# Moving the token and weight forms, the first residual adds and a late load in the block of 1024 tokens

## Chip, core and metric

The kernel runs on one core of a Trainium2 chip, as one program. The metric is the device time of one execution in microseconds, taken as the median of several runs. The engines are TensorE (PE, matrix products), VectorE (DVE), ScalarE (ACT), GpSimd (POOL) and SyncE (SP); each works through its own queue of instructions in order. Transfers are issued from SP's and POOL's queues.

## What is computed

The kernel is one block of a bidirectional encoder over 2048 tokens and 16 meta tokens of width 1024: attention and a Fourier mix from one input projection, then the part that matters here, a feed-forward net with a residual and a last norm:

```python
m = rms_norm(h, g_mlp[i])
h = h + jnp.square(jax.nn.relu(m @ w_up[i])) @ w_down[i]      # w_up 1024x4096, w_down 4096x1024
return rms_norm(h, g_final)[:, N_META:]
```

All of it is float32. A product of two float32 matrices is made from three products of halves: each operand is split into a rounded high half and a low remainder, and high x high, high x low and low x high are summed in PSUM.

## The kernel before

A split (`Split.__call__`) is two instructions: a cast on ACT that makes the high half (line 65) and a subtraction on DVE that makes the low half (line 66). `mm3` issues the three products (lines 75 to 77). So every operand of PE passes through ACT and then DVE. In the names below `h` and `l` stand for the halves: `ah`, `al` of activations, `wh_dn`, `wl_dn` of down weights, `wuh`, `wul` of up weights, `bfh`, `bfl` (or `bf` for both) of tokens, and in the down phase `bh`, `bl` of down weights.

The tokens are worked in blocks. The feed-forward net of blocks 0 and 1 (512 tokens each) runs in 8 groups of 512 hidden units: `up(b, grp)` makes four tiles of activations, each with a relu and a square on ACT and a split; `down(b, grp, halves)` multiplies them with four weight tiles for each half of the output and adds the four PSUM banks (`pdn`) to the residual rows `h` on DVE. The down weights come through a ring of three raw tiles (`wr`).

The last 1024 tokens are one block with another scheme: the 2x2 block product is done with seven products instead of eight, in the order `ORDER = "1265734"`. Operands are sums and differences of quarters ("forms"). On the weights' side the generator `up_weights()` yields the forms of one group of 512 hidden units: 1 and 2 straight from the loaded tiles R0 and R1, 6 and 5 from the sums `us2` and `us1`, 7 from a difference written in R0, then 3 and 4. On the tokens' side `b_form(name, ...)` splits the quarters `b11`, `b21`, `b12`, `b22` or differences of them (`minus`) once for all groups. The quarters come from `flips()`, which transposes the normalised rows through PSUM (`pmt`), with evictions on ACT (line 1107).

The transition into this block (lines 1154 to 1181) writes: `up(1, 7)` with the transposes between its steps, then four forms of the first weights, `b_form` 1 and 2, the first half of `down(1, 7)`, forms 5, the second half, forms 6, the last norm of block 1, and forms 7, 3 and 4. Then comes the up phase, 8 groups of seven products (`ux`, `uy`); `keep` stores activations and their sums to `s_d` in DRAM through SP (line 1220). After it the down phase runs 4 groups of seven products (`dx`, `dy`). Its operands come from `down_operands()`, two forms ahead: `a` forms from `s_d` (`stationary`), `b` forms from `w_down` (`load`), in the first group through POOL's queue and later through SP's. After the products of each form, `add(t)` adds four banks to the residual rows `hs` on DVE (line 1411). `load_h(i)` loads four residual rows of 512 KB each (line 1194); the second four (`hs1`) are first added to at form 5. The forms of products 6 and 7 continue in the same banks as product 1, so a bank's add must be done before its next product.

A scheduler of the tile framework sets the order on each engine, from the order in which the code is written and from when it reckons that inputs are there. `tc.issue_after(ins)` makes what is written inside it stand behind the instruction `ins` in the queue of `ins`'s engine.

Of the kernel before, what the change touches and what calls it, by code (L numbers as in the profile page):

```python
# [2 lines left out]

# [1 line left out]

# [7 lines left out]
AF = mybir.ActivationFunctionType  # L13
ALU = mybir.AluOpType
# [4 lines left out]
P = 128  # L19
# [32 lines left out]
def f32v(ap):  # L52
    return ap.bitcast(F32)


class Split:
# [5 lines left out]
    def __call__(self, hi, lo, src, scale=None):  # L62
        nc = self.nc
        if scale is None:
            nc.scalar.copy(hi, src)  # L65
            nc.vector.tensor_tensor(lo, src, f32v(hi), op=ALU.subtract)  # L66
        else:
            nc.scalar.activation(hi, src, AF.Copy, scale=scale)  # L68
            nc.vector.scalar_tensor_tensor(lo, src, scale, f32v(hi), op0=ALU.mult, op1=ALU.subtract)


def mm3(nc, out, a, b, first, last, chain=False):
# [7 lines left out]
def ins_of(x):  # L80
    return getattr(x, "ins", x)
# [49 lines left out]
def encoder_block(ctx: ExitStack, tc: tile.TileContext, x, meta, w_in, w_f,  # L131
                  w_out, w_up, w_down, g_fin, g_cols, g_rows, c_id, c_rope, c_dft, c_even, c_odd, c_rem, out):
    nc = tc.nc
# [281 lines left out]
    def drain(*gens):  # L415
        gens = list(gens)
        while gens:
            for g in list(gens):
                try:
                    next(g)  # L420
                except StopIteration:
                    gens.remove(g)
# [48 lines left out]
    for j in range(LAST + 1):  # L471
# [16 lines left out]
        else:  # L488
# [11 lines left out]
            a = 0  # L500
# [620 lines left out]
    def b_form(name, tiles, src):  # L1121

        BF[name] = tuple([t[:, i] for t in half for i in range(t.shape[1])] for half in tiles)
        k = 0
        for hi, lo in zip(*tiles):
            n = hi.shape[1]
            split(hi, lo, src[:, k:k + n])
            k += n
# [25 lines left out]
    fl = flips()  # L1154
    for _ in up(1, 7):
        next(fl, None)
    drain(fl)
    UW = up_weights()
    ready = [next(UW) for _ in range(4)]
    b_form("1", in_ey(0), b11)  # L1160
    b_form("2", in_ey(1), b21)
    drain(down(1, 7, (0,)))
    minus(b11, b12, b11)
    minus(b22t, b22, b11)
# [22 lines left out]

    FIRST = []
    hs = []

    def load_h(i):
        HS = ey.tile([P, 4, D], F32, name=f"hs{i}", tag=f"e{i}")
# [23 lines left out]
    for g in range(8):  # L1216
        X, Y, p1, u2, p5, C = ({} for _ in range(6))

        def keep(name, p, t):
            nc.sync.dma_start(s_d[g // 2][:, ORDER.index(name), 2 * (g % 2) + p], t)  # L1220

        for name in ORDER:
            hi, lo = ready.pop(0)
# [140 lines left out]
            yield form("4", t4)  # L1364

    gfin = [dn.tile([P, 512], F32, name=f"gf{i}", tag=f"gf{i}") for i in range(2)]
    for i in range(2):
        nc.sync.dma_start(gfin[i], g_fin[i * 512:(i + 1) * 512].rearrange("(o d) -> o d", o=1).broadcast_to([P, 512]))
    junks = [dn.tile([P, 512], F32, name=f"ej{i}", tag=f"ej{i}") for i in range(2)]
    DO = down_operands()  # L1370
    ready = [next(DO)]
    load_h(1)
    halves = (slice(0, 512), slice(512, 1024))
    sums = [small.tile([P, 2], F32, name=f"ess_{t}", tag="hss", bufs=8) for t in range(8)]
    WHERE = {"1": (0, 0), "2": (0, 0), "6": (0, 1), "5": (4, 1), "7": (4, 1), "3": (0, 1), "4": (4, 0)}
# [13 lines left out]
    for g in range(4):  # L1389
        X, Y = {}, {}  # L1390
        last = g == 3
        for name in ORDER:
# [20 lines left out]
            if not (last and name == "4"):  # L1413
                for t in range(4):
                    products(t)
                if "b" not in RING:
                    sp.release()
                    dr = Lines(tc.alloc_tile_pool(name="dr", bufs=1, side="right", reuse_waits="tile"), small)
                    RING["b"] = dr, 10
                    ready.append(next(DO))  # L1420
                w = next(DO, None)
                if w is not None:
                    ready.append(w)
                for t in range(4):
                    add(t)
                    if last and name == "2":
                        square(t, 0)
                    if last and name in "73":
                        square(o0 + t, 1)
                    if last and name == "3":  # L1430
                        store(t)
            else:
                for t in range(4):
                    products(t)
                    add(t)
                    square(4 + t, 0)
                    store(4 + t)
# [105 lines left out]
```

## Time and profile before

| | us |
|---|---|
| median of 3 runs | 2359.55 |
| lowest and highest | 2357.9, 2360.73 |
| the profiled execution | 2355.83 |
| its span, first to last instruction | 2354.0 |
| mean granted clock of TensorE, share of full | 0.991 |

The profile gives for each engine when it was busy and, where it stood idle, what it waited for. PE is the engine to look at first here. The part that the change touches begins at about 1690 us (second block's last group), the up phase of the last block runs from about 1709 to 2043 us, and its down phase from there to the end.

### The profile page before, as it was taken

The numbers are of one execution on the slowest core, as the hardware profiler recorded it, in microseconds if no ns is written. First come the engines' busy times: TensorE is split into PE (matmuls) and PEld (weight loads), VectorE is DVE, ScalarE is ACT, GpSimd is POOL, SyncE is SP. The second block draws the span as 40 slices with busy tenths as digits, with TensorE's granted clock in tenths as the row PEclk, the third lists the DMA queues.
The fourth block names the chain that finished last, engine by engine and source line by source line (L and its number), as shares of the span: only waits on it lengthen the run. The fifth ranks groups of instructions, "written<-read, shape, count | busy, mean of one in ns | idle before, by whom it ended". The sixth has DMA issues, their size and how long they took to land. (4 is left out here: it accounts for less than half of the span.)

```text
span 2354.0 us, 30528 instructions
## 1 busy us (share of the span) xinstructions
PE 2301.2 (98%) x10790; PEld 1882.8 (80%) x10790; DVE 1738.9 (74%) x2803; ACT 1292.8 (55%) x2427; POOL 173.6 (7%) x211
## 2 busy tenths in 40 slices
PE   8999989999899999999999999999999999999998
PEld 7889877677678888788878788888778888788886
DVE  5435668988877976977887987885695646597786
ACT  6434345544575655765675665664665555453333
POOL 2212120001110000200000000000000000100000
PEclk9999999999899999999999999999999999999999
DMA  6334152334543222433242353223534444865442
GB/s 212 103 106 118 46 168 68 113 114 147 187 123 100 85 81 68 122 120 109 70 151 86 112 193 105 72 81 126 179 112 170 144 165 152 318 199 164 129 134 81
DMA packets 173418, 302.08 MB, mean 128 GB/s; under 512 B 14688, under 2 KB 59456, under 8 KB 173136
## 3 DMA queue, kind: packets, MB, share of 16 engines
q1 hardware_dynamic: 154928, 259.49, 33.7%
q0 software_dynamic: 18336, 40.64, 5.8%
q8 instruction: 85, 1.39, 0.2%
q14 instruction: 69, 0.57, 0.1%
HBM read 226.37 MB, written 73.70 MB: 127 GB/s over the span
## 5 line engine op out<-in xcount | busy, mean ns | idle before, releaser
L75 PE MATMUL pdn<-wh_dn,ah 128*128 128x512 f32 x512 | 201.0, 394 | 2.7 <-ACT ah L65 2.7
L75 PE MATMUL pup<-mT,wh_up 128*128 128x512 f32 x512 | 201.7, 395 | 0.6 <-ACT mT L68 0.6
L76 PE MATMUL pdn<-wl_dn,ah 128*128 128x512 f32 x512 | 200.6, 392 | 0.0
L76 PE MATMUL pup<-mT,wh_up 128*128 128x512 f32 x512 | 200.4, 391 | 0.0
L77 PE MATMUL pup<-mT,wl_up 128*128 128x512 f32 x512 | 199.6, 392 | 0.0
L77 PE MATMUL pdn<-wh_dn,al 128*128 128x512 f32 x512 | 199.4, 391 | 0.0
L733 ACT ACTIVATE S<-S 128x512 f32<-128x512 f32 (+1 forms) x260 | 161.3, 630 | 59.8 <-DVE S L727 59.5
L691 ACT COPY S<-s 128x512 f32<-128x512 f32 (+1 forms) x272 | 158.2, 584 | 63.8 <-PE s L77 58.9
L727 DVE TENSOR_TENSOR S<-S,mb 128x512 f32<-128x512 f32 (+1 forms) x272 | 180.9, 683 | 11.9 <-ACT mb L720 11.8
L698 DVE TENSOR_TENSOR M<-M,S 128x512 f32<-128x512 f32 (+1 forms) x240 | 164.8, 687 | 32.2 <-ACT S L691 30.0
L65 ACT CAST wh_up<-wr_up 128x512 fp32r<-128x512 f32 x128 | 79.2, 622 | 152.8 <-PE pup L76 80.5
L66 DVE TENSOR_TENSOR wl_up<-wr_up,wh_up 128x512 fp32r<-128x512 f32 x128 | 87.6, 687 | 75.0 <-ACT wh_up L65 72.7
L65 ACT CAST wh_dn<-wr_dn 128x512 fp32r<-128x512 f32 x128 | 79.5, 621 | 93.4 <-PE pdn L77 50.1
L66 DVE TENSOR_TENSOR pl<-S,ph 128x512 fp32r<-128x512 f32 x180 | 123.4, 686 | 9.0 <-ACT ph L65 8.2
L75 PE MATMUL s<-q,kt 128*128 128x512 f32 (+1 forms) x272 | 126.6, 466 | 2.2 <-ACT S L691 1.2
L754 DVE TENSOR_TENSOR acc<-acc,S 128x512 f32<-128x512 f32 x180 | 123.1, 684 | 0.6 <-ACT S L733 0.2
L65 ACT CAST ah<-a 128x1024 fp32r<-128x1024 f32 x56 | 58.4, 1048 | 112.9 <-issue 62.1
L65 ACT CAST ph<-S 128x512 fp32r<-128x512 f32 x180 | 111.1, 618 | 16.8 <-PE o L77 8.1
L66 DVE TENSOR_TENSOR wl_dn<-wr_dn,wh_dn 128x512 fp32r<-128x512 f32 x128 | 87.4, 686 | 43.6 <-ACT wh_dn L65 36.8
L75 PEld LDWEIGHTS pdn<-wh_dn,ah 128*128 128x128 f32 x512 | 96.5, 189 | 25.4 <-ACT ah L65 3.1
L75 PEld LDWEIGHTS pup<-mT,wh_up 128*128 128x128 f32 x512 | 96.6, 189 | 20.4 <-ACT mT L68 1.0
L77 PEld LDWEIGHTS pdn<-wh_dn,al 128*128 128x128 f32 x512 | 96.5, 188 | 20.1
(315 smaller groups left out, 6375.5 us busy)
## 6 DMA issues: line engine op xcount, KB each, us to landing
wr_up<-in_w_up_dram SPq DMA_DIRECT2D x128, 256.0 KB, 2.8
wr_dn<-in_w_down_dram SPq DMA_DIRECT2D x128, 256.0 KB, 2.6
a<-s_d SPq DMA_DIRECT2D x42, 512.0 KB, 3.7
R<-in_w_up_dram SPq DMA_DIRECT2D x16, 1024.0 KB, 5.2
s_d<-s SPq DMA_DIRECT2D x64, 256.0 KB, 2.1
d<-in_w_down_dram SPq DMA_DIRECT2D x26, 512.0 KB, 4.9
s_d<-c SPq DMA_DIRECT2D x48, 256.0 KB, 2.0
h<-h_d SPq DMA_DIRECT2D x20, 512.0 KB, 5.6
```

Source lines behind the costliest of these rows:

```text
L65: nc.scalar.copy(hi, src)
L66: nc.vector.tensor_tensor(lo, src, f32v(hi), op=ALU.subtract)
L75: nc.tensor.matmul(out, a[0], b[0], start=first, stop=False, skip_group_check=chain)
L76: nc.tensor.matmul(out, a[0], b[1], start=False, stop=False, skip_group_check=chain)
L77: nc.tensor.matmul(out, a[1], b[0], start=False, stop=last, skip_group_check=chain)
L691: nc.scalar.copy(S[:rows], ps[:rows])
L698: nc.vector.tensor_tensor(M[:rows], M[:rows], S[:rows], op=ALU.max)
L727: nc.vector.tensor_tensor(S, S, s["mb"][:rows], op=ALU.subtract)
L733: nc.scalar.activation(p, S, AF.Exp, scale=ISQ)
L754: nc.vector.tensor_tensor(acc, acc, p, op=ALU.add)
```

## The change

There are three parts. First, the third and fourth form of the first weights (6 and 5, with their sums) and the token forms 1 and 2 are queued behind the last split of `up(1, 7)`: behind its cast in ACT's queue and behind its subtraction in DVE's. `Split` keeps its last two instructions for that. The first two forms stay as they were, and `acts_done` is taken before the remaining transposes are written. Second, `load_h(1)` and the loads of the last gain are queued behind the last `keep` store of the up phase, in SP's queue. Third, in the first down group the adds of products 1, 2 and 6 are queued behind the subtraction of the newest operand split.

```diff
--- before.py
+++ after.py
@@ -1,5 +1,5 @@
 import math
-from contextlib import ExitStack
+from contextlib import ExitStack, nullcontext
 
 import numpy as np
 
@@ -62,11 +62,12 @@
     def __call__(self, hi, lo, src, scale=None):
         nc = self.nc
         if scale is None:
-            nc.scalar.copy(hi, src)
-            nc.vector.tensor_tensor(lo, src, f32v(hi), op=ALU.subtract)
+            a = nc.scalar.copy(hi, src)
+            b = nc.vector.tensor_tensor(lo, src, f32v(hi), op=ALU.subtract)
         else:
-            nc.scalar.activation(hi, src, AF.Copy, scale=scale)
-            nc.vector.scalar_tensor_tensor(lo, src, scale, f32v(hi), op0=ALU.mult, op1=ALU.subtract)
+            a = nc.scalar.activation(hi, src, AF.Copy, scale=scale)
+            b = nc.vector.scalar_tensor_tensor(lo, src, scale, f32v(hi), op0=ALU.mult, op1=ALU.subtract)
+        self.last = ins_of(a), ins_of(b)
 
 
 def mm3(nc, out, a, b, first, last, chain=False):
@@ -1154,11 +1155,14 @@
     fl = flips()
     for _ in up(1, 7):
         next(fl, None)
+    UW = up_weights()
+    acts_done = split.last
     drain(fl)
-    UW = up_weights()
-    ready = [next(UW) for _ in range(4)]
-    b_form("1", in_ey(0), b11)
-    b_form("2", in_ey(1), b21)
+    ready = [next(UW) for _ in range(2)]
+    with tc.issue_after(acts_done[0]), tc.issue_after(acts_done[1]):
+        ready += [next(UW) for _ in range(2)]
+        b_form("1", in_ey(0), b11)
+        b_form("2", in_ey(1), b21)
     drain(down(1, 7, (0,)))
     minus(b11, b12, b11)
     minus(b22t, b22, b11)
@@ -1187,6 +1191,7 @@
 
     FIRST = []
     hs = []
+    kept = []
 
     def load_h(i):
         HS = ey.tile([P, 4, D], F32, name=f"hs{i}", tag=f"e{i}")
@@ -1217,7 +1222,7 @@
         X, Y, p1, u2, p5, C = ({} for _ in range(6))
 
         def keep(name, p, t):
-            nc.sync.dma_start(s_d[g // 2][:, ORDER.index(name), 2 * (g % 2) + p], t)
+            kept[:] = [ins_of(nc.sync.dma_start(s_d[g // 2][:, ORDER.index(name), 2 * (g % 2) + p], t))]
 
         for name in ORDER:
             hi, lo = ready.pop(0)
@@ -1364,12 +1369,12 @@
             yield form("4", t4)
 
     gfin = [dn.tile([P, 512], F32, name=f"gf{i}", tag=f"gf{i}") for i in range(2)]
-    for i in range(2):
-        nc.sync.dma_start(gfin[i], g_fin[i * 512:(i + 1) * 512].rearrange("(o d) -> o d", o=1).broadcast_to([P, 512]))
     junks = [dn.tile([P, 512], F32, name=f"ej{i}", tag=f"ej{i}") for i in range(2)]
     DO = down_operands()
     ready = [next(DO)]
-    load_h(1)
+    with tc.issue_after(kept[-1]):
+        load_h(1)
+        load_gfin(2, gfin)
     halves = (slice(0, 512), slice(512, 1024))
     sums = [small.tile([P, 2], F32, name=f"ess_{t}", tag="hss", bufs=8) for t in range(8)]
     WHERE = {"1": (0, 0), "2": (0, 0), "6": (0, 1), "5": (4, 1), "7": (4, 1), "3": (0, 1), "4": (4, 0)}
@@ -1421,8 +1426,10 @@
                 w = next(DO, None)
                 if w is not None:
                     ready.append(w)
+                behind = split.last[1]
                 for t in range(4):
-                    add(t)
+                    with tc.issue_after(behind) if g == 0 and name in "126" else nullcontext():
+                        add(t)
                     if last and name == "2":
                         square(t, 0)
                     if last and name in "73":
```

ACT's queue at the last activations of block 1, before (`r_1_7_f` are the tiles of activations, `ah_1_7_f` their casts; `wuh6` and `wuh5` are weight forms, `bf0` is token form 1):

```order
L65 CAST ah_1_7_0_16519<-r_1_7_0_16516 128x512
L65 CAST wuh6_0_16560<-us2_0_16557 128x1024
L964 ACTIVATE r_1_7_1_16523<-pup_1_7_1_16265 128x512
L65 CAST wuh5_0_16564<-us1_0_16556 128x1024
L1107 ACTIVATE b22_16262<-pmt_3_6_16504,cols_94 128x512
L1107 ACTIVATE b22_16262<-pmt_3_7_16510,cols_94 128x512
L965 ACTIVATE r_1_7_1_16523<-r_1_7_1_16523 128x512
L65 CAST bf0_16568<-b11_16259 128x1024
L65 CAST ah_1_7_1_16526<-r_1_7_1_16523 128x512
```

and after:

```order
L65 CAST ah_1_7_0_16519<-r_1_7_0_16516 128x512
L965 ACTIVATE r_1_7_1_16523<-pup_1_7_1_16265 128x512
L65 CAST wh_dn_1_7_0_2_16624<-wr_dn_1_7_0_2_16622 128x512
L966 ACTIVATE r_1_7_1_16523<-r_1_7_1_16523 128x512
L65 CAST wh_dn_1_7_0_3_16642<-wr_dn_1_7_0_3_16640 128x512
L1108 ACTIVATE b22_16262<-pmt_3_6_16504,cols_94 128x512
L1108 ACTIVATE b22_16262<-pmt_3_7_16510,cols_94 128x512
L65 CAST ah_1_7_1_16526<-r_1_7_1_16523 128x512
```

The casts of forms 6, 5 and 1 have left the place between `ah_1_7_0` and `ah_1_7_1`; two casts of down weights have come in.

DVE's queue at the same place, before (`al_1_7_f` are the low halves of the activations):

```order
L66 TENSOR_TENSOR wl_dn_1_7_0_1_16607<-wr_dn_1_7_0_1_16604,wh_dn_1_7_0_1_16606 128x512
L1088 TENSOR_TENSOR us1_0_16556<-R0_0_16544,R1_0_16546 128x1024
L66 TENSOR_TENSOR wul2_0_16553<-R1_0_16546,wuh2_0_16552 128x1024
L1089 TENSOR_TENSOR us2_0_16557<-us1_0_16556,R0_0_16544 128x1024
L1092 TENSOR_TENSOR R0_0_16544<-R0_0_16544 128x4x256
L66 TENSOR_TENSOR al_1_7_0_16520<-r_1_7_0_16516,ah_1_7_0_16519 128x512
L66 TENSOR_TENSOR wul6_0_16561<-us2_0_16557,wuh6_0_16560 128x1024
L66 TENSOR_TENSOR wul5_0_16565<-us1_0_16556,wuh5_0_16564 128x1024
L1094 TENSOR_TENSOR us2_0_16557<-R1_0_16546,us2_0_16557 128x1024
L66 TENSOR_TENSOR bf0_16568<-b11_16259,bf0_16568 128x1024
L66 TENSOR_TENSOR al_1_7_1_16527<-r_1_7_1_16523,ah_1_7_1_16526 128x512
```

and after:

```order
L66 TENSOR_TENSOR wl_dn_1_7_0_1_16607<-wr_dn_1_7_0_1_16604,wh_dn_1_7_0_1_16606 128x512
L66 TENSOR_TENSOR wul2_0_16553<-R1_0_16546,wuh2_0_16552 128x1024
L66 TENSOR_TENSOR al_1_7_0_16520<-r_1_7_0_16516,ah_1_7_0_16519 128x512
L66 TENSOR_TENSOR wl_dn_1_7_0_2_16625<-wr_dn_1_7_0_2_16622,wh_dn_1_7_0_2_16624 128x512
L66 TENSOR_TENSOR wl_dn_1_7_0_3_16643<-wr_dn_1_7_0_3_16640,wh_dn_1_7_0_3_16642 128x512
L66 TENSOR_TENSOR al_1_7_1_16527<-r_1_7_1_16523,ah_1_7_1_16526 128x512
L66 TENSOR_TENSOR al_1_7_2_16534<-r_1_7_2_16530,ah_1_7_2_16533 128x512
L66 TENSOR_TENSOR al_1_7_3_16541<-r_1_7_3_16537,ah_1_7_3_16540 128x512
L1089 TENSOR_TENSOR us1_0_16556<-R0_0_16544,R1_0_16546 128x1024
L66 TENSOR_TENSOR bf0_16568<-b11_16259,bf0_16568 128x1024
L1090 TENSOR_TENSOR us2_0_16557<-us1_0_16556,R0_0_16544 128x1024
L66 TENSOR_TENSOR bf0_16568<-b11_16259,bf0_16568 128x1024
```

The sums `us1`, `us2`, the difference in R0, the subtractions of forms 6 and 5 and those of `bf0` and `bf1` now stand behind `al_1_7_3`; the difference in R0 and the second use of `us2` stand further back still, behind the differences for form 6 and among the last norm's products. On PE, ten products of form 5 (`uy5`) now stand ahead of the products of the second output half's low weights, where before they came later. From the first product that reads `bf7_3` to the first product of the second group there are 66 matmuls on PE in the new order.

DVE's queue at the start of the down phase, before (`hs0` are the first four residual rows, `al2`, `bl2` and so on the operands of form 2; line 1330 makes differences of weights):

```order
L1411 TENSOR_TENSOR hs0_19023<-hs0_19023,dx_0_0_19181 128x512
L1411 TENSOR_TENSOR hs0_19023<-hs0_19023,dx_0_1_19194 128x512
L1411 TENSOR_TENSOR hs0_19023<-hs0_19023,dx_0_2_19207 128x512
L66 TENSOR_TENSOR al2_0_0_19161<-a2_0_0_19152,ah2_0_0_19160 128x1024
L1411 TENSOR_TENSOR hs0_19023<-hs0_19023,dx_0_3_19220 128x512
L66 TENSOR_TENSOR al2_0_1_19163<-a2_0_1_19154,ah2_0_1_19162 128x1024
L66 TENSOR_TENSOR bl2_0_0_19240<-d21_0_0_19156,bh2_0_0_19239 128x1024
L66 TENSOR_TENSOR bl2_0_1_19242<-d21_0_1_19158,bh2_0_1_19241 128x1024
L1411 TENSOR_TENSOR hs0_19023<-hs0_19023,dy2_0_0_19291 128x512
L1330 TENSOR_TENSOR d11_0_0_19164<-d12_0_0_19249,d11_0_0_19164 128x1024
```

and after:

```order
L66 TENSOR_TENSOR bl2_0_0_19240<-d21_0_0_19154,bh2_0_0_19239 128x1024
L66 TENSOR_TENSOR bl2_0_1_19242<-d21_0_1_19156,bh2_0_1_19241 128x1024
L1335 TENSOR_TENSOR d11_0_0_19162<-d12_0_0_19249,d11_0_0_19162 128x1024
L1335 TENSOR_TENSOR d11_0_1_19164<-d12_0_1_19251,d11_0_1_19164 128x1024
L1335 TENSOR_TENSOR t2_0_0_19261<-d22_0_0_19253,d11_0_0_19162 128x1024
L1335 TENSOR_TENSOR d12_0_0_19249<-d22_0_0_19253,d12_0_0_19249 128x1024
L1335 TENSOR_TENSOR t2_0_1_19262<-d22_0_1_19255,d11_0_1_19164 128x1024
L66 TENSOR_TENSOR bl6_0_0_19276<-t2_0_0_19261,bh6_0_0_19275 128x1024
L66 TENSOR_TENSOR al6_0_0_19272<-a6_0_0_19257,ah6_0_0_19271 128x1024
L66 TENSOR_TENSOR bl6_0_1_19284<-t2_0_1_19262,bh6_0_1_19283 128x1024
L66 TENSOR_TENSOR al6_0_1_19280<-a6_0_1_19259,ah6_0_1_19279 128x1024
L1416 TENSOR_TENSOR hs0_19023<-hs0_19023,dx_0_0_19181 128x512
```

The splits of form 2 stand ahead of all adds, and so do the differences and splits of form 6. In POOL's queue the loads of `a5` and `a7`, which wait for buffers that `al2` frees, keep their order.

## Rows read from the trace of the kernel before

**Rows 1.** The page, part 1: busy time of each engine, its share of the span, number of instructions.

```profile
PE 2301.2 (98%) x10790; PEld 1882.8 (80%) x10790; DVE 1738.9 (74%) x2803; ACT 1292.8 (55%) x2427; POOL 173.6 (7%) x211
```

**Rows 2.** The waits of PE, all from 1640 to 2344 us: engine, product and line, what it waited for, then us in total, times, longest.

```profile
PE pdn L75 <- ACT ah L65: 2.7, 1, 2.7
PE dy L76 <- DVE bl L66: 2.1, 1, 2.1
PE dx L75 <- ACT ah L65: 1.9, 1, 1.9
PE ux L76 <- DVE bf L66: 0.8, 1, 0.8
```

**Rows 3.** The timeline of PE around the largest wait: start us, duration us, engine, line, operation, output<-inputs, how many in a row; in brackets the idle time before it and what ended it.

```profile
1702.00 0.39 PE L77 MATMUL pdn<-wh_dn,al 128*128 128x512 f32 x1
1705.07 0.79 PE L75 MATMUL pdn<-wh_dn,ah 128*128 128x512 f32 x1 [2.68 <-ACT ah L65]
...
1708.75 0.40 PE L75 MATMUL pdn<-wh_dn,ah 128*128 128x512 f32 x1
```

**Rows 4.** Windows of 10 us: stretch, its length, busy us (and instructions) of PE, PE's weight loads, DVE, ACT and POOL, then granted TensorE clock, busy share of the DMA engines, GB/s.

```profile
1700.00:1710.00 10.00, 7.32 (x30) 5.64 (x29) 9.86 (x11) 10.00 (x16) 0.00 (x0) 0.83 0.00 0
1710.00:1720.00 10.00, 10.00 (x46) 8.25 (x46) 10.00 (x13) 8.20 (x17) 0.00 (x0) 1.00 0.16 54
1740.00:1750.00 10.00, 9.09 (x39) 6.92 (x38) 9.39 (x11) 4.26 (x6) 1.52 (x2) 1.00 0.45 156
2040.00:2050.00 10.00, 7.86 (x35) 6.17 (x34) 6.12 (x7) 0.00 (x0) 1.07 (x2) 1.00 1.04 415
2050.00:2060.00 10.00, 8.27 (x37) 6.51 (x35) 8.51 (x10) 2.95 (x4) 0.00 (x0) 1.00 0.35 137
```

**Rows 5.** The timeline of ACT ahead of the cast that ended the wait of the third group (columns as there).

```profile
1698.88 0.61 ACT L65 CAST ah<-r 128x512 fp32r<-128x512 f32 x1
1699.39 1.05 ACT L65 CAST wuh<-us 128x1024 fp32r<-128x1024 f32 x1
1700.34 0.60 ACT L964 ACTIVATE r<-pup 128x512 f32<-128x512 f32 x1
1700.83 1.05 ACT L65 CAST wuh<-us 128x1024 fp32r<-128x1024 f32 x1
...
1702.91 0.65 ACT L965 ACTIVATE r<-r 128x512 f32<-128x512 f32 x1
1703.43 1.06 ACT L65 CAST bf<-b 128x1024 fp32r<-128x1024 f32 x1
1704.37 0.65 ACT L65 CAST ah<-r 128x512 fp32r<-128x512 f32 x1
```

**Rows 6.** The timeline of PE later in the transition: the wait for form 7, and the second group's first product (the forms' products are named ux, uy; weights wuh, wul; tokens bf).

```profile
1749.23 0.50 PE L76 MATMUL ux<-bf,wuh 128*128 128x512 f32 x1 [0.85 <-DVE bf L66]
...
1767.31 0.39 PE L75 MATMUL ux<-bf,wuh 128*128 128x512 f32 x1
```

**Rows 7.** The timeline of PE at the start of the down phase.

```profile
2044.75 1.07 PE L75 MATMUL dy<-bh,ah 128*128 128x512 f32 x4
2047.96 0.50 PE L76 MATMUL dy<-bl,ah 128*128 128x512 f32 x1 [2.15 <-DVE bl L66]
...
2060.14 0.50 PE L75 MATMUL dx<-bh,ah 128*128 128x512 f32 x1 [1.88 <-ACT ah L65]
```

**Rows 8.** The waits of DVE in the transition, 1706.9 to 1752.6 us (columns as in the second group).

```profile
DVE wl_dn L66 <- ACT wh_dn L65: 1.4, 1, 1.4
DVE h L1013 <- POOL rs_m L187: 1.3, 3, 0.4
```

**Rows 9.** The timeline of DVE in the transition: first sum of the weights, one split of 128x512, residual adds, a pair of large splits, the gain's products, the first sum of the up phase.

```profile
1695.62 1.22 DVE L1088 TENSOR_TENSOR us<-R,R 128x1024 f32<-128x1024 f32 x1 [0.70 <-DMA R<-in_w_up_dram]
...
1709.68 0.69 DVE L66 TENSOR_TENSOR al<-r,ah 128x512 fp32r<-128x512 f32 x1
...
1715.49 2.47 DVE L990 TENSOR_TENSOR h<-h,pdn 128x512 f32<-128x512 f32 x4
...
1719.02 2.35 DVE L66 TENSOR_TENSOR bf<-b,bf 128x1024 fp32r<-128x1024 f32 x2
...
1735.71 2.74 DVE L1013 SCALAR_TENSOR_TENSOR h<-h,rs_m,gfin 128x512 f32<-128x512 f32 x4 [0.40 <-POOL rs_m L187]
...
1752.57 1.28 DVE L1258 TENSOR_TENSOR c<-uy,p 128x512 f32<-128x512 f32 x2
```

**Rows 10.** The timeline of DVE in the down phase: an add that waits for a product, the splits `bl2`, the first add on the second four residual rows.

```profile
2042.23 0.69 DVE L1411 TENSOR_TENSOR hs<-hs,dx 128x512 f32<-128x512 f32 x1 [2.03 <-PE dx L77]
...
2046.69 2.35 DVE L66 TENSOR_TENSOR bl<-d,bh 128x1024 fp32r<-128x1024 f32 x2
...
2078.11 1.28 DVE L1411 TENSOR_TENSOR hs<-hs,dy 128x512 f32<-128x512 f32 x2
```

**Rows 11.** The timeline of ACT in the down phase: the casts that `bl2` needs.

```profile
2037.12 1.99 ACT L65 CAST bh<-d 128x1024 fp32r<-128x1024 f32 x2
```

**Rows 12.** DMA issues from 2035 to 2055 us: output<-input, queue, operation, how many, KB each, median us from issue to landing.

```profile
a<-s_d POOLq DMA_DIRECT2D x5, 512.0 KB, 11.1
...
gf<-in_g_final_dram SPq DMA_DIRECT2D x2, 256.0 KB, 15.0
```

**Rows 13.** The timeline of the POOL queue: the issues of `a6` (two) and the first of `a5`.

```profile
2035.74 1.65 POOL L1301 DMA_DIRECT2D a<-s_d  x3
```

## Prediction

> **What bounds the kernel now.** I read the busy table first: TensorE (PE) is busy 98% of the span [rows 1], so only time in which PE stands still can be won. The list of what PE waits for from 1640 us on, the part of the program that the change touches, comes next [rows 2]: it names 7.5 us in four places. The third view is PE's own timeline at those places.
>
> The largest lies in the second block's last down products. PE waits 2.68 us for a ScalarE (ACT) cast, `ah_1_7_1` [rows 3]. After it nine matmuls take from 1705.07 to 1708.75, 3.68 us [rows 3], and the granted clock of that slice is 0.83 [rows 4]: part of it ran at 1.2 GHz instead of 2.4. At PE's full pace of 0.2265 us a matmul (the same nine are 2.04 us) the slow clock cost 1.64 us. The last matmul ahead of the wait starts at 1702.00, so the next was due at 1702.23 and the wait itself is 2.84 us: 4.5 us for the place. The ACT timeline shows why: two casts of weight forms and one of a token form stand ahead of `ah_1_7_1` (the cast at 1704.37) [rows 5].
>
> The second place is 0.85 us at 1749.23, behind VectorE (DVE) [rows 6]. The third and fourth are 2.15 us at 2047.96 and 1.88 us at 2060.14, in the down phase [rows 7]. The granted clock stays at 1.00 there [rows 4], so those two cost only themselves.
>
> The fact on which I rest most is another: in the transition DVE is nearly a bottleneck too. It is busy 10.00 of 10 us in 1710 to 1720 and 9.39 in 1740 to 1750 [rows 4], and from 1706.9 to 1752.6 it waits 2.7 us in all [rows 8].
>
> **Part 1, forms behind the last activations.** On ACT the order is now `ah_1_7_1`, `ah_1_7_2`, `ah_1_7_3`, and only then the casts of the forms. Ahead of `ah_1_7_1` are left two weight casts, a relu, a square and a pair of evictions; from the spacing of such instructions in the ACT timeline I put its end at 1703.2. PE then waits 1.0 us instead of 2.84. A wait of 2.15 us elsewhere left the clock alone [rows 4, 7], so I take the 1.64 us as gone: **3.5 us won here**.
>
> The price falls on DVE. Before, while ACT made the activations, DVE did `us1`, `us2`, a difference in R0, weight residuals and the first token forms, from 1695.62 on [rows 9]. Now they stand behind `al_1_7_3`. Each of the two last activations takes ACT 1.53 us (relu 0.49, square 0.52, cast 0.51, start to start) [rows 5], so `ah_1_7_3` ends at 1706.3 and `al_1_7_3`, 0.69 more, at 1707.0. DVE stands idle for about 6 us before that. From 1707.0 to the first sum of the new phase (`c11`, 1752.57 before) the new order has on DVE 29 instructions of 128x1024, 16 of 128x512, 8 products with the gain and 8 small ones. Durations [rows 9]: a pair of large ones takes 2.35 and one 1.22, so one more adds 1.13; four of 128x512 take 2.47 and one 0.69, so one more adds 0.59; gain products likewise 0.68. The sum is 29 x 1.13 + 16 x 0.59 + 8 x 0.68 + 8 x 0.15 (an estimate for the small ones) = 48.8 us. With no wait at all `c11` starts at 1755.8, **3.2 us later than before**.
>
> PE depends on this: `bf7_3`, the low half of form 7, lies two large instructions ahead of `c11`, so it is there at about 1753.6. From its first use 66 matmuls lead to the second group's first product: 66 x 0.2265 = 14.9 us, so 1768.5. Before, that product started at 1767.31 [rows 6]. The 3.5 us won on PE are lost again, and the floor of the stretch is **+1.2 us**. Above the floor come DVE's own waits. The one for the last down weight, 1.43 us before [rows 8], stays: its load waits for a buffer that DVE frees, and moves along. About 0.8 us is new: the residual adds of the second down half wait for products that PE, by its own waits on the way (1.0 above, then at form 5, which now stands ahead of the second half's weight residuals, 1.5 for the high half and 3.0 for the low one), delivers 0.8 us after DVE gets there. Of the 1.3 us of waits for the norm [rows 8] I keep half, as the statistics now run in pairs. Sum: 1.2 + 1.4 + 0.8 + 0.6 = **+4.0 us**, with bounds of +1.2 (DVE never waits) and +5.2 (these, and two evictions of the first products at about 0.6 each, as the casts in rows 5 take). After this PE is never idle until 2045, so nothing absorbs the delay.
>
> A rule weighed against rows: two large DVE instructions in a row take 2.35 us, not twice 1.22 [rows 9]. The Trainium skill (VectorE: DVE Perf Modes, "The TRN2 errata") gives an fp32 operation on two tensors (N+151)/0.96 ns, which is the 1.22 us of the single rows. Priced by it back to back, the 45 plain instructions would take 4 us more and the kernel would come out near 2363.7; the rows of pairs decide against that.
>
> **Part 2, residual adds behind the next operands.** Before, `al2` and `bl2` stand among adds that wait for dx products, as at 2042.23, so that `bl2` starts at 2046.69 [rows 10] and PE waits until 2047.96 [rows 7]. Their casts are long done (2037.12 plus 1.99) [rows 11]. Now the four run back to back from 2038.7, 4 x 1.13, ending at 2043.3; PE wants them at 2045.7, four matmuls after 2044.75. The **2.15 us go**. Nine large ones follow (`d11`, `t2`, `d12`, `bl6`, `al6`), ending at 2053.5; the first dx add ends at 2054.1. PE, 2.15 us earlier, reaches form 6 at 2056.0, which needs that add's bank and `ah6`. Both are there 1.9 us or more ahead, so the **1.88 us go too**. Late next could be `al6`, if its loads land late: they are issued from 2035.74 to 2037.4 [rows 13] and such loads take 11.1 us to land [rows 12], so 2048.5, against a need at 2050.1 and 2052.4. I take -4.0 us; the bounds are -4.0 and -2.1 (the second wait stays).
>
> **Part 3, second rows and gains loaded late.** Nothing computes here. Four loads of 512 KB leave the stretch around 2010 and come behind the last store, where the gains were issued (2039), with the gains now behind them on SP. Transfers run at 415 GB/s in 2040 to 2050 and fall to a third of that in 2050 to 2060 [rows 4]: the work known there ends near 2053, and 2.1 MB more, 5 us, are through by about 2058. The first add on these rows stood at 2078.11 [rows 10] and comes 4 us earlier now: 16 us of cover. The gains are used at the very end. Cost 0; were the cover gone, the add would wait up to those 5 us.
>
> A rule that speaks against it: loads in this stretch take 11.1 to 15.0 us to land [rows 12]. The Trainium skill (DMA: Bandwidth & Descriptors, "Issuing engines are not separate DMA queues") says that transfers of all issuing engines share the same 16 engines and interleave. If by that the late rows held up `al6`'s loads for their whole 5 us, these would land at 2053.5, the dx adds would come 1 to 3 us later, and the sum would grow by 1 us at most.
>
> **The sum.** +4.0 - 4.0 + 0 = 0.0 us. For the profiled execution (2355.83 us, span 2354.0) that is 2355.8 again; the median of the runs shown lies 3.7 us higher, so I forecast **2359.6 us, no change**. What a measurement of this kernel can tell from no change is 0.2%, 4.7 us.
>
> **The rivals.** *PE's gain holds* (faster). If DVE's longer queue did not reach PE, the transition would be 3.5 us shorter, and with part 2 the kernel would take 2359.55 - 3.5 - 4.0 = 2352 us. It decides at `bf7_3`, which has to be there by 1746. For it speaks that PE alone would be ready; against it, that 48.8 us of work from 1707.0 on are 8 us too much.
>
> *The clock falls again* (slower). The waits at form 5, 1.5 and 3.0 us with two matmuls between them, are together longer than the 2.68 us after which the clock fell [rows 3]. If it falls, PE's second down half is 1.6 us later, DVE's adds, which stand ahead of forms 3, 7 and 4, as much, and the rest of the norm's waits stays: 4.0 + 1.6 + 0.7 = +6.3. With part 2 at its lower bound that gives 2359.55 + 6.3 - 2.1 = 2363.8; with part 2 in full 2361.9, with two evictions more up to 2365. It decides at a wait of some 2.7 us ahead of form 5's low half.
>
> *Part 2 does not do what it says.* If DVE waits for `al6`'s loads, with the adds queued behind it, PE waits for banks instead of casts: part 2 gives 0 to -2 us, and the kernel takes 2361.6 to 2363.6, with the transition at its upper bound 2364.8.
>
> **How the numbers follow.** The sum as it stands: 0.49 (its own bounds, +1.2 - 4.0 and +5.2 - 2.1, are 2356.8 to 2362.7). PE's gain holds: 0.18. The clock falls: 0.20, part 2 fails: 0.13; about half of these two ends over 2364.3. So faster by over 0.2% has 0.18, slower 0.17, and what is left, 0.65, lies within. The range runs from 2354 to 2365.5: it takes in the sum's bounds and nearly all of the second and third rival, and leaves out most of the first.
>
> **What would show it.** In the changed profile: PE's wait at `ah_1_7_1` near 1.0 us and no slow matmuls behind it; DVE idle for 6 us before 1707; PE waiting for `bf5` near 1720 and for DVE or ACT again from 1745 to 1760; the second group's first product near 1771.3; no wait of PE from 2045 to 2060. A second group that starts before 1767 would prove the debt on DVE wrong; a wait for dx or dy banks, for `al6` or for hs would prove part 2 or 3 wrong.

## The result and the profile after

The changed kernel takes 2362.22 us (median of 21 runs, 2360.18 to 2365.07) against 2359.55 us before (21 runs, 2356.16 to 2362.87): ratio 1.0014, 95% interval 1.0008 to 1.0020. That is 2.7 us more, inside the 0.2% that was set as no change, and inside the range; the interval lies above 1, so a loss of about 0.1% is real. The two profiled executions lie further apart than that, with spans of 2354.0 and 2362.9: the one of before (2355.83 us) is faster than all 21 timed ones, the one after (2364.69) is the third slowest. What differs between executions of one kernel turned out to be part of the answer. Medians and ratios below leave out two executions that took far longer than all others, 5319.62 us in e1 and 3290.57 us in e12.

What PE waits for in the changed kernel from 1640 us on (columns as in [rows 2]):

```profile
PE uy L77 <- DVE bf L66: 3.1, 2, 2.7
PE dx L76 <- ACT bh L65: 2.9, 1, 2.9
PE ux L76 <- ACT p L1252: 2.7, 2, 2.1
PE pdn L76 <- ACT ah L65: 1.2, 1, 1.2
PE uy L76 <- ACT bf L65: 1.1, 1, 1.1
```

The wait at `ah_1_7_1` is down to 1.2 us, as forecast. In its place stand waits for form 5 (`uy` for `bf`, 2.7 and 1.1 us), for evictions (`p`, 2.1 us), and in the down phase one of 2.9 us at form 6.

The windows of the changed kernel that answer to [rows 4] (columns as there; the granted clock is third from the end):

```profile
1700.00:1710.00 10.00, 8.81 (x44) 7.03 (x43) 5.03 (x7) 9.87 (x17) 0.00 (x0) 1.00 0.19 52
...
1720.00:1730.00 10.00, 6.16 (x19) 4.31 (x18) 10.00 (x12) 3.61 (x8) 0.00 (x0) 0.71 0.09 28
...
1750.00:1760.00 10.00, 7.78 (x26) 5.69 (x25) 8.45 (x10) 6.54 (x8) 1.78 (x2) 0.83 0.47 153
...
2060.00:2070.00 10.00, 7.09 (x30) 5.50 (x29) 8.43 (x10) 7.18 (x8) 1.06 (x2) 0.95 1.02 399
2070.00:2080.00 10.00, 10.00 (x41) 8.14 (x40) 9.69 (x12) 1.21 (x2) 1.06 (x2) 0.88 0.75 236
```

The clock holds in 1700 to 1710, where it was 0.83 before. But it is 0.71 in 1720 to 1730 and 0.83 in 1750 to 1760, then 0.95 and 0.88 behind the down phase's wait. PE's timeline shows the wait that goes with each fall, and at 1776.19 the first product of the second group:

```profile
1702.02 0.48 PE L76 MATMUL pdn<-wh_dn,ah 128*128 128x512 f32 x1
...
1704.83 0.50 PE L76 MATMUL pdn<-wh_dn,ah 128*128 128x512 f32 x1 [1.19 <-ACT ah L65]
...
1722.87 0.73 PE L76 MATMUL uy<-bf,wuh 128*128 128x512 f32 x2 [1.11 <-ACT bf L65]
1726.34 0.80 PE L77 MATMUL uy<-bf,wuh 128*128 128x512 f32 x1 [2.73 <-DVE bf L66]
```

```profile
1754.05 0.50 PE L76 MATMUL ux<-bf,wuh 128*128 128x512 f32 x1 [2.06 <-ACT p L1252]
...
1776.19 0.39 PE L76 MATMUL ux<-bf,wuh 128*128 128x512 f32 x1
...
2067.58 0.47 PE L76 MATMUL dx<-bh,ah 128*128 128x512 f32 x1 [2.91 <-ACT bh L65]
```

The second group was forecast near 1771.3. This execution reaches the transition 1.25 us later than the one of before (1702.02 against 1700.77), so the second group comes 7.6 us later where 4.0 were forecast.

DVE's timeline in the transition and at the start of the down phase:

```profile
1704.81 0.69 DVE L66 TENSOR_TENSOR al<-r,ah 128x512 fp32r<-128x512 f32 x1 [0.98 <-ACT ah L65]
...
1708.44 0.69 DVE L66 TENSOR_TENSOR al<-r,ah 128x512 fp32r<-128x512 f32 x1 [1.12 <-ACT ah L65]
1709.05 1.22 DVE L1089 TENSOR_TENSOR us<-R,R 128x1024 f32<-128x1024 f32 x1
...
1757.36 1.22 DVE L66 TENSOR_TENSOR bf<-b,bf 128x1024 fp32r<-128x1024 f32 x1
...
1761.98 1.28 DVE L1263 TENSOR_TENSOR c<-uy,p 128x512 f32<-128x512 f32 x2
```

```profile
2049.72 0.69 DVE L1258 TENSOR_TENSOR s<-c,s 128x512 f32<-128x512 f32 x1 [3.14 <-DMA s_d<-s]
...
2063.34 1.23 DVE L66 TENSOR_TENSOR al<-a,ah 128x1024 fp32r<-128x1024 f32 x1 [1.57 <-DMA s_d<-s]
...
2066.75 2.48 DVE L1416 TENSOR_TENSOR hs<-hs,dx 128x512 f32<-128x512 f32 x4
```

`al_1_7_3` is the row at 1708.44; the first of the deferred sums starts at 1709.05, the low half `bf7_3` at 1757.36 and `c11` at 1761.98. From the first product of the last down group (1702.02) to `c11` it is 59.96 us; before, from 1700.77 to the last row of [rows 9] (1752.57), it was 51.80. In the down phase the last sum waits until 2049.72 and `al6` until 2063.34, and the four dx adds queued behind `al6` start at 2066.75; PE's form 6 starts at 2067.58. The list of waits puts this down to a cast (`bh`), but form 6's casts of `bh` had ended by 2061.8; by the rows the first add came last, which gives the bank back.

### The profile page after: what moved, and what is told of

The parts are those of the page before. It is cut to its first block, busy times and chain, and to the rows that moved or that the text cites. A ratio compares the mean times of both kernels' runs of the same rounds, so it can differ in the third digit from the quotient of the medians.

```text
span 2362.9 us, 30538 instructions
## 1 busy us (share of the span) xinstructions
PE 2305.7 (98%) x10790; PEld 1885.1 (80%) x10790; DVE 1737.8 (74%) x2803; ACT 1292.5 (55%) x2427; POOL 173.8 (7%) x211
## 4 chain that ended last, share of the span: by engine, by line
PE 74%; DVE 4%; DMA 4%; issue 3%; ACT 2%; POOL 1%; DVEq 0%; POOLq 0%; SPq 0%; ACTq 0%
PE pdn L77 5%; PE pdn L78 5%; PE pdn L76 5%; PE pup L76 5%; PE pup L78 5%; PE pup L77 5%; PE ux L76 2%; PE ux L77 2%; PE ux L78 2%; PE s L76 2%; PE s L77 2%; PE s L78 2%; PE o L749 2%; PE dx L76 2%; PE dx L77 2%
```

## The experiments

Each was timed against the kernel before on the same chip. The table has all twelve; the texts follow.

| run | what it is | median us | before beside it | ratio, 95% interval |
|---|---|---|---|---|
| e1 | part 1 alone | 2365.47 | 2358.88 | 1.0030 (1.0017 to 1.0042) |
| e2 | part 2 alone | 2351.87 | 2358.88 | 0.9970 (0.9958 to 0.9981) |
| e3 | part 3 alone | 2358.64 | 2358.88 | 0.9998 (0.9989 to 1.0007) |
| e4 | parts 2 and 3 | 2354.03 | 2358.88 | 0.9977 (0.9968 to 0.9986) |
| e5 | part 1, ACT's queue only | 2361.77 | 2357.86 | 1.0012 (1.0003 to 1.0021) |
| e6 | part 1, DVE's queue only | 2369.99 | 2357.86 | 1.0050 (1.0037 to 1.0064) |
| e7 | weight forms only, ACT only | 2359.36 | 2357.86 | 1.0005 (0.9996 to 1.0014) |
| e8 | e7 with part 2 | 2353.60 | 2357.86 | 0.9981 (0.9972 to 0.9989) |
| e9 | forms behind `ah_1_7_1`, ACT only | 2356.41 | 2357.93 | 0.9996 (0.9987 to 1.0005) |
| e10 | e9 with part 2 | 2352.15 | 2357.93 | 0.9973 (0.9961 to 0.9984) |
| e11 | e2 again | 2351.86 | 2357.93 | 0.9973 (0.9962 to 0.9984) |
| e12 | e4 again | 2353.22 | 2357.93 | 0.9977 (0.9967 to 0.9987) |

From the timelines of the profiled executions I also took three stretches. Two begin at the first product of `pdn` in the last down group: one ends at the first sum `c11` (the transition on DVE), one at PE's first product of the second group (the transition on PE, the same 264 matmuls in every kernel). The third goes from PE's first product of the down phase to the start of its last matmul, 1344 matmuls each time. The last column tells whether the granted clock was below 1.00 in a window of the down phase's first 40 us:

| | to `c11`, us | to the second group, us | down phase on PE, us | clock there |
|---|---|---|---|---|
| before | 51.80 | 66.54 | 309.17 | full |
| changed | 59.96 | 74.16 | 309.21 | fell |
| e1 | 60.54 | 74.74 | 310.63 | fell |
| e2 / e11 | 52.22 / 51.52 | 66.94 / 66.22 | 304.41 / 304.41 | full, full |
| e3 | 52.81 | 67.51 | 310.65 | fell |
| e4 / e12 | 52.27 / 51.58 | 66.99 / 66.30 | 305.78 / 304.96 | full, full |
| e5 | 58.00 | 71.16 | 309.16 | full |
| e6 | 63.10 | 77.34 | 312.23 | fell twice |
| e7 / e8 | 54.07 / 54.16 | 68.26 / 68.40 | 310.67 / 305.28 | fell / full |
| e9 / e10 | 51.58 / 51.30 | 65.78 / 65.55 | 309.15 / 305.77 | full, full |

**e1 to e4: the parts one by one.** Against the changed kernel, e1 takes parts 2 and 3 back, e2 parts 1 and 3, e3 parts 1 and 2, e4 part 1:

```diff
 part 1 back:
+    drain(fl)
     UW = up_weights()
-    acts_done = split.last
-    drain(fl)
-    ready = [next(UW) for _ in range(2)]
-    with tc.issue_after(acts_done[0]), tc.issue_after(acts_done[1]):
-        ready += [next(UW) for _ in range(2)]
-        b_form("1", in_ey(0), b11)
-        b_form("2", in_ey(1), b21)
+    ready = [next(UW) for _ in range(4)]
+    b_form("1", in_ey(0), b11)
+    b_form("2", in_ey(1), b21)
 part 2 back:
-                    with tc.issue_after(behind) if g == 0 and name in "126" else nullcontext():
-                        add(t)
+                    add(t)
 part 3 back:
+    for i in range(2):
+        nc.sync.dma_start(gfin[i], g_fin[i * 512:(i + 1) * 512].rearrange("(o d) -> o d", o=1).broadcast_to([P, 512]))
 ...
-    with tc.issue_after(kept[-1]):
-        load_h(1)
-        load_gfin(2, gfin)
+    load_h(1)
```

> Part 1 alone (forms behind the last activations). Debt theory: the whole loss of the change sits in the transition, because VectorE stands idle ahead of al_1_7_3 and PE then waits at form 5 and at form 7, each time with a fall of the clock; the kernel takes 3 to 6 us more than before (2362.5 to 2365.5), the first sum c11 about 8 us later against the first product of the transition, and the two waits at 2047 and 2060 stay. Rival, late rows: part 1 is neutral (within 1 us of before) and the loss of the whole change comes from part 3.

> Part 2 alone (first residual adds behind the next operands, rows loaded as before). Debt theory: it wins 1 to 4 us (2355.5 to 2358.5): both waits of 2.15 and 1.88 us go, and only what al6's loads and the stores of the last activations hold up stays, with no late rows beside them. Rival, late rows: it wins the full 4 us, since only the late rows stood against it. If it wins nothing, the adds behind al6 are themselves the new wait.

> Part 3 alone (second rows and gains loaded behind the last store). Debt theory: no change, within 1 us of before; the rows land by about 2058 and are first needed after 2074. Rival, late rows: 2 to 3 us slower, with loads of a6, a5 and the stores landing later in 2040 to 2055 and PE waiting longer at 2048 and 2060 than the 2.15 and 1.88 us of before.

> Parts 2 and 3 together, the transition as before. Debt theory: 1 to 2 us faster than before (the whole change's down phase was about 1 us shorter than before from the last sums of the up phase on), so 2357.5 to 2358.5, with a wait for a dx bank of 1 to 3 us at form 6 that is released by the residual adds. Rival, late rows: 2 to 3 us slower than part 2 alone.

Part 1 alone loses 6.6 us (3 to 6 expected; the interval of its ratio is 4.0 to 9.9 us), part 2 alone wins 7.0 (1 to 4 expected), part 3 alone does nothing that can be measured, and parts 2 and 3 win 4.9, more than the 1 to 2 us expected. Part 1 with parts 2 and 3 is +6.6 - 4.9 = +1.7; the whole, +2.7, lies well within the noise of that sum. So the loss is part 1's; the rival (late rows) falls, since e3's interval ends at +1.7 us and it said 2 to 3. Part 1's waits of PE:

```profile
PE uy L77 <- DVE bf L66: 3.1, 2, 2.7
PE ux L76 <- ACT p L1252: 2.6, 2, 2.1
PE dy L77 <- DVE bl L66: 2.1, 1, 2.1
PE dx L76 <- ACT ah L65: 1.9, 1, 1.9
```

They are those of the changed kernel at forms 5 and 7, and the old two at the start of the down phase. In e2 PE never waits there; its windows (columns as in [rows 4]):

```profile
2040.00:2050.00 10.00, 10.00 (x46) 8.29 (x45) 10.00 (x10) 3.13 (x4) 0.53 (x1) 1.00 1.04 414
2050.00:2060.00 10.00, 10.00 (x46) 8.29 (x45) 9.73 (x12) 5.72 (x6) 2.12 (x4) 1.00 0.79 275
2060.00:2070.00 10.00, 10.00 (x46) 8.29 (x45) 9.77 (x12) 3.90 (x4) 0.53 (x1) 1.00 0.70 239
```

Part 2 won more than the 4 us which the waits cost in [rows 7], for two reasons. The first is that a wait costs PE more than the idle time in its row. Where the two waits stand and the clock holds (before, e5, e9), PE's down phase takes 309.15 to 309.17 us; without them (e2, e11) it takes 304.41. That is 4.75 us, not 2.15 + 1.88. The second stands in executions whose down phase is as before, e3 and e1. After the same two waits their clock falls (e3's window, then e1's):

```profile
2060.00:2070.00 10.00, 8.12 (x29) 6.23 (x28) 10.00 (x10) 6.73 (x7) 2.11 (x4) 0.83 0.48 160
```

```profile
2060.00:2070.00 10.00, 8.12 (x34) 6.40 (x33) 9.79 (x11) 4.74 (x5) 0.00 (x0) 0.95 0.19 76
2070.00:2080.00 10.00, 10.00 (x40) 8.11 (x40) 10.00 (x10) 4.47 (x6) 2.12 (x4) 0.88 0.77 257
```

Of the seven executions with these two waits (before, e1, e3, e5, e6, e7, e9) the clock fell in four. One fall adds 1.5 us (310.63 to 310.67 in e1, e3, e7), and the two of e6 add 3.1. Part 2 takes away the waits and so also this chance: 4.75 and four sevenths of about 1.5 us make some 5.6 us by my estimate. The medians give 7.0 (e2), 6.1 (e11), 5.8 (e8 against e7), 4.6 (e4 against e3) and 4.3 (e10 against e9).

**e5 and e6: which queue.** One of the two edges is left out:

```diff
-    with tc.issue_after(acts_done[0]), tc.issue_after(acts_done[1]):
+    with tc.issue_after(acts_done[0]):      # e5; e6 has acts_done[1]
```

> Part 1 with the edge on ScalarE's queue alone: the casts of the forms stay behind ah_1_7_3, but VectorE is free to make us1, us2 and the difference in R0 before al_1_7_0, three instructions of 3.4 us. Debt theory: the low half of form 5 comes 2.3 us earlier, so its wait of 2.7 us in part 1 shrinks to under 1 us and the clock does not fall there; c11 comes 3 to 4 us earlier than in part 1 alone; 1 to 3 us slower than before instead of 7. Rival, order on PE (form 5 hoisted ahead of the second half's low weights is what costs, whatever VectorE does): as slow as part 1 alone, 6 to 8 us.

> Part 1 with the edge on VectorE's queue alone: VectorE stands as idle as in part 1 (the sums behind al_1_7_3), while on ScalarE some casts of form 1 stay ahead of the activations. Debt theory: as slow as part 1 or slower, 6 to 9 us over before, with the same waits at forms 5 and 7. Rival (ScalarE's order is what costs): near before.

With DVE free again the loss shrinks from 0.30% to 0.12% (3.9 us by the medians, 1 to 3 expected), though PE's order still has form 5 ahead of the second half's low weights. DVE makes the sums early (two rows), and the transition to `c11` is 2.5 us shorter than in e1 (3 to 4 expected):

```profile
1697.09 1.22 DVE L1089 TENSOR_TENSOR us<-R,R 128x1024 f32<-128x1024 f32 x1 [0.83 <-DMA R<-in_w_up_dram]
...
1700.62 1.22 DVE L1093 TENSOR_TENSOR R<-R 128x1024 f32<-128x1024 f32 x1
```

The wait for form 5 did not shrink as I said, but by little, from 2.73 to 2.53 us, and the clock fell behind it once (window 1720 to 1730 at 0.83 instead of 0.71):

```profile
1724.46 0.65 PE L77 MATMUL uy<-bf,wuh 128*128 128x512 f32 x1 [2.53 <-DVE bf L66]
```

So the sign and the order of e5 between before and e1 hold, the mechanism in its details half. With the edge on DVE alone the kernel is the slowest of all, 12.1 us over before where 6 to 9 were expected. DVE waits for activations, with nothing else to do:

```profile
1701.74 0.69 DVE L66 TENSOR_TENSOR al<-r,ah 128x512 fp32r<-128x512 f32 x1 [2.44 <-ACT ah L65]
1706.10 0.69 DVE L66 TENSOR_TENSOR al<-r,ah 128x512 fp32r<-128x512 f32 x1 [3.67 <-ACT ah L65]
```

**e7 and e8: move less.** Only the weight forms 6 and 5 stay inside, behind the last activation on ACT; `b_form` 1 and 2 are as before. e8 adds part 2.

```diff
+    with tc.issue_after(acts_done[0]):
+        ready += [next(UW) for _ in range(2)]
+    b_form("1", in_ey(0), b11)
+    b_form("2", in_ey(1), b21)
```

> Only the weight forms 6 and 5 behind the last activation, on ScalarE's queue alone; the token forms 1 and 2 where they were and VectorE as busy as before: in its order only the two subtractions of these forms move back, and seven of nine products of form 5 stand late on PE again. Debt theory: the wait at ah_1_7_1 shrinks by some 1.5 us, no new wait over 1.5 us at form 5, so 1 to 4 us faster than before. Rival, order on PE: no change or slower by some us, since the first products of form 5 still stand early.

> The transition of the kernel with only the weight forms moved, together with part 2 and without part 3. If the stages add up as they did for the change (part 1 +7.0, parts 2 and 3 -4.9, all +2.7), this is the gain of that transition plus part 2's -7.0: 2348 to 2351, faster than before and than the change.

A miss for both. e7 has no gain: two casts of token form 1 are ahead of `ah_1_7_1` on ACT, and the wait is still 2.40 us. So e8 has what part 2 gives and no more, 2353.60 us where 2348 to 2351 were expected:

```profile
1706.45 0.50 PE L76 MATMUL pdn<-wh_dn,ah 128*128 128x512 f32 x1 [2.40 <-ACT ah L65]
```

**e9 and e10: an earlier edge.** `up` keeps the split of each activation, and the forms stand behind the second one on ACT alone. e10 adds part 2.

```diff
             split(*hl, r)
             acts.append(hl)
+            MT[b, grp, f] = split.last
...
-    acts_done = split.last
+    acts_done = MT[1, 7, 1]
+    with tc.issue_after(acts_done[0]):
```

> All four forms behind the second of the last activations (ah_1_7_1) and on ScalarE's queue alone; the third and fourth activation mix with the forms again. VectorE has us1, us2 and the difference in R0 early, and its first splits of the forms 3 us earlier than with the edge at ah_1_7_3. Debt theory: PE waits 1.1 us at ah_1_7_1 without a fall of the clock, up to 1 us more for ah_1_7_3, and 1 to 1.5 us for form 5's low half, too short for a fall there: 0 to 3 us faster than before. If the clock falls all the same at form 5 or at form 7, 2 to 4 us slower, as with the edge at ah_1_7_3 on ScalarE alone.

> The same transition with part 2 and without part 3. If the stages add up: e9's difference to before plus part 2's -7.0, so 2348 to 2351 by the debt theory, 2353 to 2355 if the clock falls in the transition.

PE's waits are now two short ones, and the clock holds:

```profile
1703.34 0.50 PE L76 MATMUL pdn<-wh_dn,ah 128*128 128x512 f32 x1 [1.17 <-ACT ah L65]
...
1707.71 0.50 PE L76 MATMUL pdn<-wh_dn,ah 128*128 128x512 f32 x1 [1.26 <-ACT ah L65]
```

And yet `c11` comes after 51.58 us, 0.2 us less than before, the second group 0.8 us earlier (1.0 in e10), and the kernel is at 0.9996. e10 takes 2352.15 us, between the two ranges that were expected. The two short waits are together 2.43 us, little less than the 2.68 of before, so what e9 takes away is above all the fall of the clock. The 4.5 us that the wait and the slow clock seemed to cost were for the most part not on the path that sets the end. e12 shows the same from the other side. There the transition is that of before, the wait is 2.84 us, the clock in 1700 to 1710 happens to hold (1.00), and `c11` comes after 51.58 us:

```profile
1704.83 0.50 PE L76 MATMUL pdn<-wh_dn,ah 128*128 128x512 f32 x1 [2.84 <-ACT ah L65]
```

```profile
1700.00:1710.00 10.00, 6.16 (x28) 4.14 (x27) 9.86 (x11) 10.00 (x16) 0.00 (x0) 1.00 0.00 0
```

For comparison e2, the same transition with a wait of 2.83 us and a fall behind it:

```profile
1700.00:1710.00 10.00, 7.02 (x24) 4.74 (x23) 9.86 (x11) 10.00 (x16) 0.00 (x0) 0.83 0.00 0
```

Where the clock holds (e9, e11, e12) `c11` comes after 51.5 to 51.6 us, where it falls with the old transition (before, e2, e3, e4) after 51.8 to 52.8. The fall thus costs 0.7 us on the mean, not the 1.64 that PE loses. DVE sets the length: in before, e9 and e12 it waits 2.7, 2.3 and 2.2 us between the first product of `pdn` and `c11`, and never for a product of PE itself. No run takes the wait away and leaves DVE's work where it was, so that the wait is worth little is argued from DVE's rows and not shown.

**e11 and e12: does part 3 cost anything beside part 2?** The kernels are e2 and e4 again.

> Part 2 alone once more, beside parts 2 and 3 on the same chip. Contention theory (the late rows share the transfers of the stretch in which al6's loads land): 1.5 to 2.5 us faster than parts 2 and 3 together, and its profile has no wait over 1 us at form 6. Rival: the two are the same within 0.8 us.

> Parts 2 and 3 once more. Contention theory: 1.5 to 2.5 us slower than part 2 alone, with a wait of 1 to 3 us for a dx bank or a cast at form 6. Rival: the same as part 2 alone within 0.8 us.

Part 3 looked 2.2 us dear in e4 and 1.4 in e12, where 1.5 to 2.5 was one theory and under 0.8 the other; the intervals of the ratios overlap in both. The executions fit a small cost without proving it: PE waits 1.10 us at form 6 in e4, 0.27 in e12, not at all in e2 and e11, but 0.59 and 1.07 in e8 and e10, which have no part 3. These waits have two origins. In e4 and e12 `al6` doesn't wait, but DVE's queue begins late, behind the up phase's last sum (e4's row, then e2's):

```profile
2042.30 0.69 DVE L1255 TENSOR_TENSOR s<-c,s 128x512 f32<-128x512 f32 x1 [3.65 <-DMA s_d<-s]
```

```profile
2037.17 0.69 DVE L1255 TENSOR_TENSOR s<-c,s 128x512 f32<-128x512 f32 x1 [2.86 <-DMA s_d<-s]
```

Counted from PE's first product of the down phase that is 6.8 us in e4 and 3.6 in e2. It is 6.0 to 7.0 in all four profiled executions with part 3 and 1.6 to 5.2 in the ten without. So the traces lean to a cost of part 3 next to part 2; why the sum comes later stays open.

What the wait in e10 hangs on is settled: the residual adds, behind `al6`, which itself waits for a transfer of `s_d`, not for its own load:

```profile
2052.03 1.23 DVE L66 TENSOR_TENSOR al<-a,ah 128x1024 fp32r<-128x1024 f32 x1 [2.65 <-DMA s_d<-s]
...
2055.45 2.48 DVE L1417 TENSOR_TENSOR hs<-hs,dx 128x512 f32<-128x512 f32 x4
```

In the program `al6`'s first subtraction waits for two transfers, the load of `a6` and the store of `s4_7_1`, the last activation's sum. In the profile after, this store is issued at 2050.44 and takes 12.8 us to land, so 2063.2, and `al6` starts at 2063.34. The changed kernel has both delays: its last sum comes 7.0 us after PE's first product, and `al6` waits 1.57 us more.

```profile
2050.44 0.32 SPq L1225 DMA_DIRECT2D s_d<-s  x1
```

```profile
s_d<-s SPq DMA_DIRECT2D x1, 256.0 KB, 12.8
```

The best versions are part 2 alone (2351.86 to 2351.87 us, 0.3% faster than before) and part 2 with the transition of e9 (2352.15); they can't be told apart.

## Why the prediction came out

No change was right, the working behind it was not: part 1 cost 2.6 us more than its term and part 2 won 2 to 3 us more than its own, with opposite signs. That the sum came out near is luck: the two errors cancel.

- **Part 1, what it wins on PE.** The wait shrank to 1.19 us (forecast 1.0) and the fall of the clock behind it went, as said. That this is worth 3.5 us was wrong: with the fall gone and 0.25 us less of waiting, e9's second group comes 0.8 us earlier than before (1.2 us earlier than the mean of before, e2, e3 and e4), since DVE's work sets the length of the transition.
- **Part 1, what it costs on DVE.** The mechanism was right, its size 2.1 us too small: `c11` comes 8.2 us later against the first product of `pdn`, where the forecast's terms make 6.0 (3.2 + 1.4 + 0.8 + 0.6). 0.8 us of it lie ahead of the deferred work: the prediction gave each activation 1.53 us on ACT, from rows in which an instruction on another tile stood behind each. With relu, square and cast of one tile in a row, each starts 0.66 us after the one that it needs, and the casts are 1.8 us apart:

```profile
1704.65 0.62 ACT L965 ACTIVATE r<-pup 128x512 f32<-128x512 f32 x1
1705.31 0.63 ACT L966 ACTIVATE r<-r 128x512 f32<-128x512 f32 x1
1705.97 0.62 ACT L65 CAST ah<-r 128x512 fp32r<-128x512 f32 x1
...
1707.78 0.62 ACT L65 CAST ah<-r 128x512 fp32r<-128x512 f32 x1
```

  The work from there to `c11` was forecast as 48.8 us; measured are 52.93 us from 1709.05 to 1761.98, of which the list of DVE's waits has 3.9 (1.9 for `bfh`, 1.1 for `bf`, 0.9 for the norm). Waits of 2.8 us were forecast, and other ones: for the last down weight and for the adds DVE did not wait. Those for `bfh` go back to PE, whose late products of `pdn` hold up ACT's casts:

```profile
1735.25 0.62 ACT L65 CAST bfh<-b 128x512 fp32r<-128x512 f32 x1 [2.12 <-PE pdn L78]
```

- **The step that failed in part 1** is the choice of +4.0 over the second rival. *The clock falls again* is what happened, at form 5 as it said, and once more at form 7, for which it named no fall. It was priced at +6.3; e1 measured +6.6. That the waits at form 5 (1.11 and 2.73 us; forecast 1.5 and 3.0) would be long enough for it stood in the text, and the sum left it out. The path was wrong as well: the sum lets PE wait for `bf7_3`. By its place, two large instructions ahead of `c11`, that was there at 1758.6, but counted back 66 matmuls from 1776.19 PE got to it more than 2 us later. It had waited 2.06 us at form 7 for an eviction, which came late on ACT, and run at the slow clock behind that.

```profile
1753.41 0.58 ACT L1252 COPY p<-ux 128x512 f32<-128x512 f32 x1 [0.41 <-DVE h L1014]
```

- **Part 2.** Both old waits went, as said. The step that failed is "The granted clock stays at 1.00 there [rows 4], so those two cost only themselves." The clock held in the one execution that was profiled, and in four of seven with these waits it fell. And with the clock full the two cost 4.75 us, not 4.0. The row of a wait counts from the end that is shown for the product before: the product that started at 2047.96 was due at 2045.7, so it lost 2.3 us and not 2.15, and the first product behind a wait takes 0.50 us instead of 0.39 [rows 7]. At `ah_1_7_1` the prediction reckoned with that (2.84 for 2.68), here it did not.
- **What is late next in part 2** was right in the place (`al6`, with the adds queued behind it) and wrong in the cause: the landing of the last stores, not the load. In the changed kernel it was enough to take part 2's gain in the profiled execution: PE's down phase is 309.21 us there and 309.17 before.
- **Part 3.** Alone zero, as said (0.9998); nothing waited for the late rows. Beside part 2 it may cost some 1 to 2 us.
- **The sum against the whole.** +6.6 - 4.9 is +1.7, measured +2.7.

Two sentences on pages of the Trainium skill stood in the working. The durations by "VectorE: DVE Perf Modes" ("The TRN2 errata") are again those of single rows here (1.22 us), and the 48.8 us from pairs fit what was measured less its waits (49.0). The interleaving of transfers by the Trainium skill's "DMA: Bandwidth & Descriptors" ("Issuing engines are not separate DMA queues") neither showed a cost for part 3 beyond noise nor ruled one out.

## To carry to other kernels

A wait of the busiest engine is worth its length only if what it waits for next is not late as well: move the instructions that cause it, and check first whether the engine that feeds the stage has any idle time to take them. An edge that puts work behind an event should hold the one queue that is in the way, not each queue of that work, and no longer than needed: DVE, busy 5.03 of the 10 us from 1700 on instead of 9.86, paid for an edge that only ACT needed. On ACT alone the edge still cost 0.12% behind the fourth activation (e5) and nothing behind the second (e9). And a single profile says whether the clock fell in that execution, not whether it falls.

## What the runs showed of the hardware

After the same two waits of 2.15 and 1.88 us the granted clock fell to half (1.2 of 2.4 GHz) for some microseconds in four executions and held in three; each fall made that stage 1.5 us longer. With a wait of 2.83 us it fell in e2 (0.83 in 1700 to 1710), with one of 2.84 us it held in e12 (1.00). In the transition and at the start of the down phase, waits of 1.1 to 1.3 us with no longer one next to them were never followed by a fall. Stores of 256 KB to `s_d` issued at the end of the up phase, with 413 GB/s moving in 2050 to 2060, took 12.8 us to land in the changed kernel.
